# A hybrid decoder layer: where the gate sums, their weights' buffers and a scan's output sums stand in the heads' stage

## Chip, cores, metric

One core of a Trainium2 chip runs the whole layer as one program. The metric is the device time of one execution in microseconds (us); lower is better. Engines are named as in the profile: PE (matrix products; PEld its weight loads), DVE (vector), ACT (scalar), POOL (GpSimd), SP (the queue that issues most transfers).

## What is computed

One layer with 512 tokens and width 2048, in float32: a normalised and modulated input, one wide projection, a sliding-window attention branch, a gated DeltaNet branch, and a gated merge of the two. The change lies in the DeltaNet branch (32 value heads, in pairs that share one of 16 key heads) and in the layer's output gate, which is computed beside it:

```python
mod = jax.nn.silu(c) @ w_ada + b_ada
shift, scale, gate = jnp.split(mod[:, None, :], 3, axis=-1)
...
o = gated_delta_rule(dq, dk, dv, g, beta)
o = rms_norm(o, dn_norm_w) * jax.nn.silu(dz.reshape(B, T, DN_V_HEADS, DN_HEAD_V).astype(f32))
y_b = o.reshape(B, T, DN_VAL).astype(x.dtype) @ w_o_dn
...
return x + gate * (y @ w_out)
```

The product with `w_o_dn` is done with seven products of half-size blocks instead of eight (a Strassen-Winograd scheme). It needs sums of the four quarters of `o` (two heads by two halves of the tokens) as inputs: these are the "input sums" of the change, made by `head_sums`.

## The kernel before

Each projection is a `channel_tile` (line 254 to 256 by its helper `mm3`): 16 blocks of 128 by 128 weights against 512 tokens, each as three products of split numbers (high and low parts). A weight half is copied by ACT (`whi`, line 52) and subtracted by DVE (`wlo`, line 53); `raw` is its load on SP.

The order of everything else hangs on these tiles. After every second block `channel_tile` calls `pump()`, and this document calls one such call a **step**: 8 steps a tile. A piece of side work is a Python generator; it gets a step, issues some instructions, and says with `yield n` after how many steps it wants to go on. `go` puts a generator into the list `live`. `beside(gen, rate)` puts one into a queue that is served after the live ones: its counter grows by `rate` a step and the generator gets a turn for each whole 1.0. The instructions so issued get their place in the program's order. That order is a priority: a scheduler at build time simulates the program and gives each engine the first instruction that is ready, so that one can overtake another. Only generators wrapped in `ordered` (the gate, and the sums of `w_od` that use POOL and SP transfers) are tied behind the last matrix product before them.

`heads(wk, g)` runs for g = 0 to 15, one pair of heads each, with five tiles: the query tile (steps 1 to 8), two value tiles (9 to 16 and 17 to 24) and two output-gate tiles `z` (25 to 32 and 33 to 40). Counted from the `yield`s, a pair's work falls on these steps; numbers over 40 lie in the next pair, 40 lower:

| step | work (line) |
|---|---|
| 9 to 13 | query convolution: 3 DVE products at 10 (595), tanh at 12, DVE at 13 (602) |
| 17 to 21 | the same for the first value tile, `yv`: 595 at 18, tanh (600) at 20, 602 at 21 |
| 19 | POOL's decay masks (792, 794); loads of `qe`, `tt`, `ta`, `lab` |
| 23 | transposes of the first value tile, `ptv` (288), then ACT's copy; POOL's `qe` product (945) |
| 24, 26, 28 | `pqk` with its masks on DVE (951); `py`; `pu` |
| 25 to 31 | the second value tile: 595 at 26, 602 at 29, `ptv` at 31 |
| 33, 41 | first and second `z`: ACT writes `zh` (880) and a tanh |
| 34 to 54 | the scan in four chunks: `pv`, ACT's `vn` (1000), DVE's `vs` (1005), `pd`, `po` (1018) |
| 56, 57 | root of the norm, then two products on `osb` (1048) |
| 59, 60 | transposes `pto` and product into `z` (1055), one per head |
| 61, 65 | the four sums (1064 to 1067) into `osb`; three transfers to `oq_d` (1070) |

Buffers: `z` has two, one per head; `osb` one; the transposes, `pqk`, `py`, `pu` and `pgate` share two banks (`ptp`).

The gate runs from pair 8 on at 0.125 a step: at steps 8, 16, 24, 32 and 40 of every pair. Each of 32 turns multiplies a 128 by 1024 block of weights by a scalar and adds it to a sum (line 1637, DVE), and loads the block two turns ahead into one of two buffers `gw` (1626). Then four times a matrix product `pgate` (1645) and, one turn later, a bias (1647, 1648).

Of the kernel before, what the change touches and what calls it, by code (L numbers as in the profile page):

```python
# [7 lines left out]
F32 = mybir.dt.float32  # L8
# [3 lines left out]
ALU = mybir.AluOpType  # L12
# [4 lines left out]
P = 128  # L17
T = 512
D = 2048
KT = D // P  # L20
# [16 lines left out]
class Layer:  # L37
# [650 lines left out]

    def od_order(self):
        return [  # L690
            ("m1", 0, (0, 0)), ("m2", 1, (1, 0)), ("m5", 3, None), ("m6", 4, None), ("m7", 5, None), ("m4", 2, None),
            ("m3", 6, (1, 1)),
        ]

# [173 lines left out]
    def heads(self, wk, g):  # L868

        st = {"z": []}  # L870
        self.go(self.queries(wk, g, self.channel_tile(f"q{g}"), st), 0)
        for e in range(2):
            self.go(self.values(wk, g, e, self.channel_tile(f"v{2 * g + e}"), st), 0)
        for e in range(2):
            self.go(self.zgate(wk, self.channel_tile(f"z{2 * g + e}"), st), 0)
# [102 lines left out]
    def scan(self, wk, g, k, kT, TT, qd, M, epsq, st):  # L978
# [3 lines left out]
        osb = wk.tile([P, 2, NTB, P], F32, tag="osb", name="osb", bufs=1)  # L982
        osq = wk.tile([P, 2, NTB], F32, tag="osq", name="osq")
        S = None
        for c in range(NTB):
            if c:
# [3 lines left out]
                for e in range(2):  # L990
                    nc.vector.scalar_tensor_tensor(  # L991
                        out=r[:, e, :], in0=pp[:, e, :], scalar=self.neg_eg[:, c, 2 * g + e : 2 * g + e + 1],
                        in1=v[e][:, c, :], op0=ALU.mult, op1=ALU.add,
# [8 lines left out]
            if c < NTB - 1:  # L1002
                vs = wk.tile([P, 2, P], F32, tag="vs", name="vs", bufs=1)
                for e in range(2):
                    nc.vector.tensor_scalar(
                        out=vs[:, e, :], in0=vn[:, e, :], scalar1=self.kd[:, c, 2 * g + e : 2 * g + e + 1],
# [15 lines left out]
            if c < NTB - 1:  # L1022
# [3 lines left out]
                else:  # L1026
                    for e in range(2):
                        nc.vector.scalar_tensor_tensor(
                            out=Sn[:, e, :], in0=S[:, e, :], scalar=self.egl[:, c, 2 * g + e : 2 * g + e + 1],
                            in1=pd[:, e, :], op0=ALU.mult, op1=ALU.add,  # L1030
# [4 lines left out]
        z = st["z"]  # L1035
# [4 lines left out]
        for e in range(2):  # L1040
            nc.vector.scalar_tensor_tensor(
                out=ms[:, e, :], in0=osq[:, e, :], scalar=1.0 / P, in1=epsq, op0=ALU.mult, op1=ALU.add
# [3 lines left out]
        for e in range(2):  # L1046
            of = osb[:, e]
            nc.vector.tensor_tensor(
                out=of, in0=of, in1=ro[:, e * NTB : (e + 1) * NTB].unsqueeze(2).to_broadcast([P, NTB, P]), op=ALU.mult
            )  # L1050
        yield 2
        for e in range(2):
# [1 line left out]
            self.transpose4(pt, lambda c: osb[:, e, c, :])  # L1054
            nc.vector.tensor_tensor(out=z[e], in0=pt, in1=z[e], op=ALU.mult)
            yield 1
        yield from self.head_sums(g, z, osb.rearrange("p e c i -> p (e c i)").rearrange("p (q t) -> p q t", q=4))

    def head_sums(self, g, z, s):

        nc = self.nc
        TT, STT = nc.vector.tensor_tensor, nc.vector.scalar_tensor_tensor
        lo, hi = slice(0, 256), slice(256, 512)
        TT(out=s[:, 0], in0=z[0][:, hi], in1=z[1][:, hi], op=ALU.subtract)
        STT(out=s[:, 1], in0=s[:, 0], scalar=-1.0, in1=z[0][:, lo], op0=ALU.mult, op1=ALU.subtract)
        TT(out=s[:, 2], in0=z[0][:, lo], in1=z[0][:, hi], op=ALU.add)
        STT(out=s[:, 3], in0=s[:, 1], scalar=-1.0, in1=z[1][:, lo], op0=ALU.mult, op1=ALU.subtract)
        yield 4
        for q, src in ((slice(0, 1), z[0][:, lo].unsqueeze(1)), (slice(1, 3), z[1].rearrange("p (q t) -> p q t", q=2)), (slice(3, 7), s)):
            nc.sync.dma_start(out=self.oq_d[q, g // 2].rearrange("q p k t -> p q k t")[:, :, g % 2, :], in_=src)  # L1070


# [545 lines left out]
    def gate(self, wk):  # L1618

        nc, a = self.nc, self.a  # L1620
        acc = wk.tile([P, D], F32, name="gate_bc", bufs=1)
        ws = {}

        def load(i):
            ws[i] = wk.tile([P, 1024], F32, tag="gw", name="gw", bufs=2)
            nc.sync.dma_start(out=ws[i], in_=a["w_ada_gate"][i // 2][:, i % 2 * 1024 : i % 2 * 1024 + 1024])

        load(0)
        load(1)
        for i in range(2 * KT):  # L1630
            yield
            s = self.sc[:, i // 2 : i // 2 + 1]
            o = acc[:, i % 2 * 1024 : i % 2 * 1024 + 1024]
            if i < 2:
                nc.vector.tensor_scalar(out=o, in0=ws.pop(i), scalar1=s, scalar2=None, op0=ALU.mult)
            else:
                nc.vector.scalar_tensor_tensor(out=o, in0=ws.pop(i), scalar=s, in1=o, op0=ALU.mult, op1=ALU.add)
            if i + 2 < 2 * KT:
                load(i + 2)
        for c in range(4):  # L1640
            sl = slice(c * T, (c + 1) * T)
            b = wk.tile([P, T], F32, tag="gb", name="gb", bufs=1)
            nc.sync.dma_start(out=b, in_=a["b_gate"][sl].partition_broadcast(P))
            ps = self.ptp.tile([P, T], F32, tag="tp", name="pgate")
            nc.tensor.matmul(ps, lhsT=self.ones, rhs=acc[:, sl], start=True, stop=True)
            yield
            nc.vector.tensor_tensor(out=acc[:, sl], in0=ps, in1=b, op=ALU.add)
            nc.vector.tensor_scalar(out=acc[:, sl], in0=acc[:, sl], scalar1=0.5, scalar2=None, op0=ALU.mult)
            yield
            nc.sync.dma_start(out=self.gate_d[sl], in_=acc[0:1, sl])  # L1650
# [80 lines left out]
```

## Time and profile before

| | us |
|---|---|
| median of 3 runs | 2895.6 (2894.57 to 2895.92) |
| profiled execution, its own time | 2899.93 |
| its span, first to last instruction | 2898.1 |
| PE busy | 2835.8 |
| DVE busy | 1874.1 |
| ACT busy | 1140.0 |
| POOL busy | 272.5 |

The page's busy times are unions over the span; a line such as "PE ptv L288 <- DVE yv L602" names the instruction that stood, its line, and the one that released it. In the heads' stage the first pair's `pqk` is at 560.1 us of the span and the last one's at 1596.4; the gate's DVE work runs from 1089.3 to 1621.1.

### The profile page before, as it was taken

How to read it: one execution, taken by the hardware profiler on the slowest of the kernel's cores; microseconds unless marked ns; L12 is line 12 of the kernel's file. 1: busy time of each engine (PE TensorE's matmuls, PEld its weight loads, DVE VectorE, ACT ScalarE, POOL GpSimd, SP SyncE). 2: the span in 40 equal slices, each digit the busy share in tenths (PEclk: the TensorE clock that was granted, in tenths of full speed). 3: DMA queues.
4: the chain of work that ended last, by engine and by line, in shares of the span. 5: the costliest groups of instructions: out<-in, count | busy, mean ns of one | idle time of the engine just before them, and what ended most of it. 6: DMA issues, size and time to landing. Idle time of an engine off the chain costs nothing.

```text
span 2898.1 us, 38268 instructions
## 1 busy us (share of the span) xinstructions
PE 2835.8 (98%) x14428; PEld 2324.7 (80%) x14428; DVE 1874.1 (65%) x3020; ACT 1140.0 (39%) x2161; POOL 272.5 (9%) x266
## 2 busy tenths in 40 slices
PE   8899999999999999999999999999999999999999
PEld 6677888888888888888777888888887788788787
DVE  6765899777876656666665456665655655554565
ACT  4355333433334333333333354443344434432343
POOL 0013111101111111112010000000100100000000
PEclk9999999999999999999999999999999999999999
DMA  9756554637667778878772377676645547365575
GB/s 372 295 171 200 173 179 147 209 117 229 190 194 214 235 212 245 242 224 241 247 209 85 127 252 265 240 247 210 218 153 162 157 154 218 119 225 185 185 231 165
DMA packets 205472, 590.08 MB, mean 204 GB/s; under 512 B 74564, under 2 KB 99652, under 8 KB 154088
## 3 DMA queue, kind: packets, MB, share of 16 engines
q1 hardware_dynamic: 195080, 529.44, 53.8%
q0 software_dynamic: 10208, 58.20, 10.3%
q8 instruction: 113, 1.85, 0.3%
q14 instruction: 71, 0.58, 0.1%
HBM read 523.79 MB, written 166.40 MB: 238 GB/s over the span
## 4 chain that ended last, share of the span: by engine, by line
PE 82%; DVE 4%; issue 2%; DMA 2%; ACT 1%; POOL 0%; SPq 0%; DVEq 0%; POOLq 0%; ACTq 0%
PE mm L254 19%; PE mm L256 19%; PE mm L255 19%; PE od L255 3%; PE od L256 3%; PE od L254 3%; PE m L255 2%; PE m L256 2%; PE m L254 2%; PE S L1369 1%; DVE wlo L53 1%; PE pv L998 1%; PE po L1017 1%; PE pP L288 1%; PE O L1420 1%
## 5 line engine op out<-in xcount | busy, mean ns | idle before, releaser
L254 PE MATMUL mm<-hh,whi 128*128 128x512 f32 x2784 | 1134.4, 407 | 2.3 <-ACT whi L52 1.6
L256 PE MATMUL mm<-hh,wlo 128*128 128x512 f32 x2784 | 1091.3, 392 | 1.2 <-DVE wlo L53 1.2
L255 PE MATMUL mm<-hl,whi 128*128 128x512 f32 x2784 | 1089.0, 391 | 0.0
L53 DVE TENSOR_TENSOR wlo<-raw,whi 128x1024 fp32r<-128x1024 f32 (+1 forms) x476 | 590.2, 1242 | 411.2 <-ACT whi L52 401.1
L52 ACT CAST whi<-raw 128x1024 fp32r<-128x1024 f32 (+1 forms) x476 | 495.4, 1044 | 798.0 <-PE mm L255 676.5
L256 PEld LDWEIGHTS mm<-hh,wlo 128*128 128x128 f32 x2784 | 523.5, 188 | 115.7 <-DVE wlo L53 2.1
L254 PEld LDWEIGHTS mm<-hh,whi 128*128 128x128 f32 x2784 | 524.7, 188 | 113.1 <-issue 9.6
L255 PEld LDWEIGHTS mm<-hl,whi 128*128 128x128 f32 x2784 | 525.1, 189 | 99.8 <-issue 1.4
L255 PE MATMUL od<-wlo,oh 128*128 128x512 f32 x448 | 174.7, 390 | 1.0 <-DVE wlo L53 1.0
L254 PE MATMUL od<-whi,oh 128*128 128x512 f32 x448 | 174.9, 391 | 0.0
L256 PE MATMUL od<-whi,ol 128*128 128x512 f32 x448 | 174.4, 389 | 0.0
L792 POOL TENSOR_TENSOR E<-E,neg_g 128x512 f32<-128x512 f32 x64 | 87.4, 1365 | 493.3 <-DMA E<-g_rows 382.1
L945 POOL TENSOR_TENSOR qe<-qe,yq 128x512 f32<-128x512 f32 x32 | 46.0, 1455 | 869.4 <-DMA qe<-eg_rows 749.6
L844 DVE TENSOR_TENSOR A<-A,atmp 128x62 f32<-128x62 f32 (+30 forms) x124 | 113.1, 912 | 1.5
L837 DVE TENSOR_TENSOR atmp<-A 128x62 f32<-128x62 f32 (+30 forms) x124 | 109.5, 883 | 1.4
L255 PEld LDWEIGHTS od<-wlo,oh 128*128 128x128 f32 x448 | 84.1, 188 | 18.7 <-DVE wlo L53 1.6
L254 PEld LDWEIGHTS od<-whi,oh 128*128 128x128 f32 x448 | 84.1, 188 | 17.4 <-ACT whi L52 0.3
L256 PEld LDWEIGHTS od<-whi,ol 128*128 128x128 f32 x448 | 84.1, 188 | 17.4
L53 DVE TENSOR_TENSOR wlo<-raww,whi 128x1024 fp32r<-128x1024 f32 x56 | 68.4, 1223 | 44.1 <-ACT whi L52 44.1
L52 ACT CAST whi<-raww 128x1024 fp32r<-128x1024 f32 x56 | 58.8, 1054 | 79.4 <-PE m L256 71.8
L991 DVE SCALAR_TENSOR_TENSOR r<-pp,neg_eg,vt 128x128 f32<-128x128 f32 x96 | 29.2, 346 | 77.9 <-PE pp L988 77.6
L1393 ACT ACTIVATE sm<-sm,mx,rs 128x256 f32<-128x256 f32 (+1 forms) x128 | 71.7, 562 | 3.3 <-DVE mx L1388 3.3
(341 smaller groups left out, 3273.9 us busy)
## 6 DMA issues: line engine op xcount, KB each, us to landing
raw<-in_w_ch SPq DMA_DIRECT2D x158, 1024.0 KB
wa<-in_w_ada_ss SPq DMA_DIRECT2D x32, 1024.0 KB
od_m<-in_w_od POOLq DMA_DIRECT2D x32, 1024.0 KB, 13.5
raw<-od_m SPq DMA_DIRECT2D x32, 1024.0 KB
raw<-in_w_od SPq DMA_DIRECT2D x24, 1024.0 KB
E<-g_rows SPq DMA_DIRECT2D x64, 256.0 KB
od_m<-in_w_od SPq DMA_DIRECT2D x16, 1024.0 KB
od_m<-od_m SPq DMA_DIRECT2D x16, 1024.0 KB
```

The lines of the kernel that those rows point to most:

```text
L52: self.nc.scalar.copy(out=hi, in_=src)
L53: self.nc.vector.tensor_tensor(out=lo, in0=src, in1=hi.bitcast(F32), op=ALU.subtract)
L254: nc.tensor.matmul(ps, lhsT=wh, rhs=xh, start=first, stop=False)
L255: nc.tensor.matmul(ps, lhsT=wh, rhs=xl, start=False, stop=False)
L256: self.last_mm = nc.tensor.matmul(ps, lhsT=wl, rhs=xh, start=False, stop=last).ins
L288: self.nc.tensor.transpose(dst[:, c * P : (c + 1) * P], src_cols(c), self.ident)
L792: self.in_turn(nc.gpsimd.tensor_tensor(out=E, in0=E, in1=ng, op=ALU.add))
L837: eng.tensor_tensor(out=t, in0=A[:, m : m + 1, m + 1 :].to_broadcast([P, m, n]), in1=A[:, :m, m : m + 1].to_broadcast([P, m, n]), op=ALU.mult,
L844: eng.tensor_tensor(out=A[:, :m, m + 1 :], in0=A[:, :m, m + 1 :], in1=t, op=ALU.add)
L945: self.in_turn(nc.gpsimd.tensor_tensor(out=qf, in0=qf, in1=q, op=ALU.mult))
L991: nc.vector.scalar_tensor_tensor(out=r[:, e, :], in0=pp[:, e, :], scalar=self.neg_eg[:, c, 2 * g + e : 2 * g + e + 1], in1=v[e][:, c, :], ...
L1393: nc.scalar.activation(t, t, AF.Exp, scale=r[:, h : h + 1], bias=mx[:, h : h + 1], accum_out=den[:, h : h + 1])
```

## The change

It has three parts. `heads` sets the rate of the gate's queue to 0 at the start of each pair and to 0.22 before the second value tile, so that the gate gets turns only in steps 17 to 40; its weights get three buffers and are loaded three turns ahead, and its bias takes one of these buffers. Ten steps are put between the last transpose of a scan's output and the four sums, which then fall on steps 71 and 72 (31 and 32 of the next pair), their transfers on 75 (35). And the sums go into a tile of their own with three parts (`zs`), the fourth into `z[0]` itself; the seven inputs get a new order in `oq_d`, and `od_order` names them by it.

```diff
-            ("m1", 0, (0, 0)), ("m2", 1, (1, 0)), ("m5", 3, None), ("m6", 4, None), ("m7", 5, None), ("m4", 2, None),
+            ("m1", 0, (0, 0)), ("m2", 2, (1, 0)), ("m5", 4, None), ("m6", 5, None), ("m7", 1, None), ("m4", 3, None),
...
         st = {"z": []}
+        for q in self.side.get("gate", []):
+            q[1] = 0.0
         self.go(self.queries(wk, g, self.channel_tile(f"q{g}"), st), 0)
         for e in range(2):
+            for q in self.side.get("gate", []) if e else []:
+                q[1] = 0.22
             self.go(self.values(wk, g, e, self.channel_tile(f"v{2 * g + e}"), st), 0)
...
-        yield from self.head_sums(g, z, osb.rearrange("p e c i -> p (e c i)").rearrange("p (q t) -> p q t", q=4))
-
-    def head_sums(self, g, z, s):
+        yield 10
+        yield from self.head_sums(wk, g, z)
+
+    def head_sums(self, wk, g, z):
...
+        s = wk.tile([P, 3, 256], F32, tag="sums", name="zs", bufs=1)
         TT(out=s[:, 0], in0=z[0][:, hi], in1=z[1][:, hi], op=ALU.subtract)
         STT(out=s[:, 1], in0=s[:, 0], scalar=-1.0, in1=z[0][:, lo], op0=ALU.mult, op1=ALU.subtract)
-        TT(out=s[:, 2], in0=z[0][:, lo], in1=z[0][:, hi], op=ALU.add)
-        STT(out=s[:, 3], in0=s[:, 1], scalar=-1.0, in1=z[1][:, lo], op0=ALU.mult, op1=ALU.subtract)
-        yield 4
-        for q, src in ((slice(0, 1), z[0][:, lo].unsqueeze(1)), (slice(1, 3), z[1].rearrange("p (q t) -> p q t", q=2)), (slice(3, 7), s)):
+        yield 1
+        TT(out=z[0][:, hi], in0=z[0][:, lo], in1=z[0][:, hi], op=ALU.add)
+        STT(out=s[:, 2], in0=s[:, 1], scalar=-1.0, in1=z[1][:, lo], op0=ALU.mult, op1=ALU.subtract)
+        yield 3
+        two = lambda x: x.rearrange("p (q t) -> p q t", q=2)
+        for q, src in ((slice(0, 2), two(z[0])), (slice(2, 4), two(z[1])), (slice(4, 7), s)):
             nc.sync.dma_start(out=self.oq_d[q, g // 2].rearrange("q p k t -> p q k t")[:, :, g % 2, :], in_=src)
...
-            ws[i] = wk.tile([P, 1024], F32, tag="gw", name="gw", bufs=2)
+            ws[i] = wk.tile([P, 1024], F32, tag="gw", name="gw", bufs=3)
...
-        load(0)
-        load(1)
+        for i in range(3):
+            load(i)
...
-            if i + 2 < 2 * KT:
-                load(i + 2)
+            if i + 3 < 2 * KT:
+                load(i + 3)
...
-            b = wk.tile([P, T], F32, tag="gb", name="gb", bufs=1)
+            b = wk.tile([P, 1024], F32, tag="gw", name="gb", bufs=3)[:, :T]
```

## The prediction

> **What bounds the kernel now.** I read the page first, then the matrix engine's waits in the stage that the change touches, then stretches cut from one query-key product (pqk) to the next, which is one pair of heads, and last the order of instructions on DVE, ACT and SP inside a pair.
>
> ```profile
> span 2898.1 us, 38268 instructions
> PE 2835.8 (98%) x14428; PEld 2324.7 (80%) x14428; DVE 1874.1 (65%) x3020; ACT 1140.0 (39%) x2161; POOL 272.5 (9%) x266
> PE 82%; DVE 4%; issue 2%; DMA 2%; ACT 1%; POOL 0%; SPq 0%; DVEq 0%; POOLq 0%; ACTq 0%
> ```
>
> PE works 98% of the span. The change takes no matrix product away, so it can only win back time in which PE waits or is slow. The waits of PE from 1033 to 1680 us (line waited for: us in total, times, longest):
>
> ```profile
> PE ptv L288 <- DVE yv L602: 11.6, 6, 2.6
> PE pto L288 <- DVE zh L1055: 2.2, 1, 2.2
> PE pto L288 <- DVE osb L1048: 1.3, 1, 1.3
> ```
>
> Six times PE stands at the transposes of the first value tile (ptv) until DVE has finished that tile's activation (yv, line 602). The stretches (length, then busy time of PE, PEld, DVE, ACT, POOL, clock, DMA):
>
> ```profile
> 763.14:830.45 67.31, 67.31 (x359) 56.04 (x358) 55.54 (x86) 24.81 (x57) 10.97 (x10) 1.00 0.66 195
> 1033.62:1172.67 139.05, 136.51 (x714) 113.29 (x714) 83.83 (x141) 50.01 (x113) 17.33 (x17) 0.99 0.79 233
> 1172.67:1241.87 69.20, 67.50 (x358) 55.96 (x358) 42.78 (x72) 24.95 (x57) 8.61 (x8) 1.00 0.81 241
> 1241.87:1310.78 68.91, 67.47 (x358) 55.94 (x358) 42.67 (x72) 25.04 (x57) 9.91 (x9) 1.00 0.72 227
> 1310.78:1380.61 69.83, 67.46 (x359) 55.96 (x358) 44.35 (x73) 25.14 (x57) 9.31 (x9) 1.00 0.83 244
> 1380.61:1449.17 68.56, 67.47 (x358) 55.95 (x358) 42.34 (x71) 25.03 (x57) 5.86 (x7) 1.00 0.78 248
> 1449.17:1520.89 71.72, 69.08 (x359) 57.22 (x358) 45.81 (x74) 26.02 (x59) 12.67 (x11) 0.98 0.74 207
> 1520.89:1595.77 74.88, 72.64 (x365) 58.68 (x364) 39.95 (x73) 23.79 (x55) 2.53 (x2) 0.98 0.28 94
> 1168.50:1173.00 4.50, 3.92 (x15) 3.37 (x16) 2.40 (x4) 1.31 (x2) 0.00 (x0) 0.62 1.01 215
> 1517.00:1521.50 4.50, 4.21 (x17) 3.66 (x18) 2.10 (x4) 1.56 (x3) 0.00 (x0) 0.62 0.92 313
> ```
>
> A pair without the gate's sums takes 67.31 us and PE never stops. With them, the seven pairs in rows two to seven take 139.05 + 69.20 + 68.91 + 69.83 + 68.56 + 71.72 = 487.27 us against 7 x 67.31 = 471.17: 16.1 us too many. 11.6 of it is the six waits. The granted clock is 0.62 over 4.5 us at two of them, 0.38 x 4.5 = 1.7 us each, 3.4 together; the rest, 1.1, is small. The ceiling of the main effect is 16.1 us, 0.56%. The eighth pair (1520.89) has 7.6 us extra: the 2.2 of the pto wait, slow clock and the gate's own matrix products.
>
> The clock drops behind waits of at most 2.6 us. The Trainium skill, "TensorE: Matmul & The Clock Gate", section "Part 1: The HAM clock gate", says that the clock halves after an idle window of about 3.4 us. By that rule the drops would not hang on these waits, and the forecast below would be 3.4 us higher; the trace has both drops right at two of the six waits, and I follow the trace. By the rule it would be 2887.3 in place of 2883.9.
>
> **The change part by part.** One pair is 40 steps of 67.31 / 40 = 1.68 us. Why L602 is late, in the pair of 1310.78 (DVE, POOL, then PE):
>
> ```profile
> 1365.88 0.69 DVE L1048 TENSOR_TENSOR osb<-osb,roy 128x512 f32<-128x512 f32 x1
> 1366.49 1.28 DVE L1637 SCALAR_TENSOR_TENSOR gate_bc<-gw,silu_c,gate_bc 128x1024 f32<-128x1024 f32 x1
> 1367.69 1.78 DVE L1048 TENSOR_TENSOR osb<-osb,roy 128x512 f32<-128x512 f32 x1
> ...
> 1374.71 1.08 DVE L1066 TENSOR_TENSOR osb<-zh 128x256 f32<-128x256 f32 x1
> 1375.71 0.68 DVE L1055 TENSOR_TENSOR zh<-pto,zh 128x512 f32<-128x512 f32 x1
> 1376.31 1.21 DVE L53 TENSOR_TENSOR wlo<-raw,whi 128x1024 fp32r<-128x1024 f32 x1
> 1377.44 0.41 DVE L1064 TENSOR_TENSOR osb<-zh 128x256 f32<-128x256 f32 x1
> 1377.78 0.68 DVE L602 SCALAR_TENSOR_TENSOR yv<-th,yv 128x512 f32<-128x512 f32 x1
> 1367.60 3.01 POOL L945 TENSOR_TENSOR qe<-qe,yq 128x512 f32<-128x512 f32 x2 [57.29 <-DMA qe<-eg_rows]
> 1378.60 0.63 PE L288 MATMUL ptv<-ident,yv 128*128 128x128 f32 x4 [2.37 <-DVE yv L602]
> ```
>
> PE is there at 1378.60 - 2.37 = 1376.23, 10.35 us after the first osb; L602 ends 12.58 after it, with a gate sum (1.20 start to start) and two input sums (1.00 and 0.34) ahead. A pair without a gate sum:
>
> ```profile
> 1021.43 1.29 DVE L1048 TENSOR_TENSOR osb<-osb,roy 128x512 f32<-128x512 f32 x2
> 1026.92 1.15 DVE L602 SCALAR_TENSOR_TENSOR yv<-th,yv 128x512 f32<-128x512 f32 x1 [0.16 <-ACT th L600]
> 1031.63 0.60 PE L288 MATMUL ptv<-ident,yv 128*128 128x128 f32 x4
> ```
>
> There L602 ends 6.64 after the first osb and PE comes 3.56 us later.
>
> *Gate sums.* None falls at step 16 any more. At 0.22 a step, counted from step 17, the first of a pair comes at steps 21, 20, 19, 17, 21, 19, 18, 17 of the eight pairs. At 21 it is written after L602, at 17 to 20 still ahead of it. *Input sums.* Ten more steps put them from step 21 to 31 and 32 in the program's order, behind both tiles' L602 (21 and 29). But the order on each engine is made by a scheduler that runs what is ready, and nothing ties these sums to their step, so I expect them right behind L602, where DVE had them in pairs without a gate sum. What they delay there is the mask of pqk at step 24; DVE has room for it, busy 42 to 46 of some 69 us in the stretches above.
>
> For the quoted pair: 12.58 - 1.34 = 11.24 with a gate sum still ahead, 10.04 with none. Against 10.35, PE waits 0.9 or nothing. The other bound is the pair at 1021.43: 6.64 and even a gate sum of 1.20 added is 2.5 us early, because once the backlog is gone L602 overtakes the second wlo. Five pairs of the waiting six have their gate sum at 17 to 20: 0 to 4.5 us left. I take 1.0, nearer to the second row, since a pair that has neither a gate sum at step 16 nor input sums ahead of L602 starts out as that pair does. Gain 16.1 - 1.0 = 15.1.
>
> The second osb above takes 1.78 instead of 0.69 us beside POOL's qe. The Trainium skill, "SBUF — State Buffer", section "SBUF: two separate sides", says that a DVE instruction with two SBUF inputs and a GpSimd instruction exclude each other for the whole instruction; the row agrees. It speaks against the new place, which lies in POOL's burst: the second rival.
>
> *Output buffers.* The sums now read z and write into z[0]; the transfers of z[0] wait for the third sum. z has two buffers, and the next pair's zh takes the first at step 33, though the transfers are written at step 35. The place of the present last transfer, behind the sums, shows what to expect (SP, ACT, DVE; then who waited for it):
>
> ```profile
> 1310.62 0.37 SPq L1070 DMA_DIRECT2D oq_d<-osb  x1
> 1325.48 0.69 ACT L880 ACTIVATE zh<-mm,dnwh 128x512 f32<-128x512 f32 x1
> 1328.35 0.48 DVE L1005 TENSOR_SCALAR vs<-vn,kd 128x128 f32<-128x128 f32 x2 [0.91 <-ACT vn L1000]
> 1331.12 0.42 DVE L1025 COPY S<-pd 128x256 f32<-128x256 f32 x1 [2.29 <-PE pd L1013]
> 1331.57 0.37 ACT L1018 COPY osb<-po 128x256 f32<-128x256 f32 x1
>   ACT osb L1018: 2.9, 1
> ```
>
> That transfer has until 1331.57 and was late once, by 2.9 us. zh is due 6.1 us earlier, so the worst pair could hold ACT for 9.0 us. Queued on ACT behind zh: its tanh, vn of the scan, the next weight cast. vs, and PE's pd behind it, have about 2.5 us to spare (idle 0.91 and part of 2.29). So 0 to 6.5 us for a pair, 0 to 97 for fifteen pairs. Fourteen of fifteen transfers met the later term and z[0]'s is ahead of most of the bytes: I take one or two pairs, 2.5 us. On SP it must get ahead of the loads that follow the products of step 26, or it stands behind these 9.6 us:
>
> ```profile
> 1316.36 4.83 SPq L932 DMA_DIRECT2D ta<-ta_d  x1
> 1321.23 4.77 SPq L933 DMA_DIRECT2D lab<-lab_d  x1
> ```
>
> *Weights of the gate sums.* Same 32 loads and the same bytes, bunched in 24 steps of 40, issued three sums ahead. DVE waited for them hardly at all:
>
> ```profile
> DVE gate_bc L1637 <- DMA gw<-in_w_ada_gate: 0.5, 1, 0.5
> ```
>
> The load-to-use distance shrinks from 16 steps (26.9 us) to 13 or 14 (about 22), in the first pair to 5 (8.4). A late one blocks DVE with wlo and the second L602 behind it: 0 to 6 us, I take 0.9. What it can save is that 0.5. The reordered rows of the scratch tensor move the same bytes in three transfers: nothing. The gate's last products still hold one of two transpose buffers at steps 19 and 20 of the eighth pair, so the 2.2 us pto wait stays; if not, it comes back with its slow clock, 0.02 x 74.88 = 1.5, together 3.7.
>
> Sum: -16.1 + 1.0 + 2.5 + 0.9 = -11.7. The profiled execution took 2899.93, so 2888.2 for it; the median of the three runs is 4.3 lower, 2895.6, and 2895.6 - 11.7 = 2883.9.
>
> **The rivals.** *A: the output buffers decide (slower).* From the point where z[0]'s transfers land more than 2.5 us after zh is due, as when the sums slip past step 26 and SP is held. For it: the one late transfer, DMA shares of 0.66 to 0.83. Against: fourteen met a term only 6.1 us later, and zh can wait in the scheduler's order. Eight pairs at 3 us on PE: 24 more than nothing, 2895.6 - 15.1 + 0.9 + 24 = 2905.
>
> *B: the gate sum meets POOL's burst ahead of L602.* Now and then it does already (min/median/max in ns):
>
> ```profile
> L1637 DVE SCALAR_TENSOR_TENSOR gate_bc<-gw,silu_c,gate_bc x30: 1265/1277/2118, 1112.4 to 1517.9; 128x1024 f32<-128x1024 f32 x30
> ```
>
> A sum at steps 17 to 20 waits for a POOL instruction, 3.01 / 2 = 1.5 us, and five pairs keep 0.9 + 1.5 = 2.4 us, less what shrinks of the other overlaps, say 1.6: 8 us, one clock drop with it. -16.1 + 9.7 + 2 = -4.4: 2891. That is also the sum by the page's rule on the shared port. Against: 3.56 us of slack in the row at 1031.63.
>
> *C: the order hardly changes*, since the scheduler hoists the sums ahead of L602 wherever its tanh is late: 2894.
>
> **How the numbers follow.** About 0.2%, 5.8 us, is what a measurement of this kernel can tell from no change. Forecast 0.57, A 0.18, B 0.15, C 0.10. The forecast's own range is 2876 (all 19.8 us back: 16.1 + 3.7) to 2890. Up to 2900 it takes in B, C and a mild A. Faster: 0.57 and two thirds of B, 0.67; same: the rest of B, and C, 0.15; slower: A, 0.18.
>
> **What would show it.** Right: the pairs after 1033 take 67.3 to 67.8 us, the ptv row is gone from PE's waits or below 2 us, the clock is 1.00 there, the four sums stand behind L602. Wrong: a row of ACT zh waiting for the oq_d transfer with PE pd waiting for vs behind it (A), ptv waits of 1 to 2 us with a stretched gate sum ahead (B), sums still ahead of L602 (C), or waits at pqk, py or pu that are not there now.

## The result, and the profile after

| | median (lowest to highest), us | against before, 95% interval |
|---|---|---|
| before, 8 runs | 2895.02 (2891.92 to 2899.24) | |
| after, 8 runs | 2883.93 (2880.12 to 2893.21) | 0.9964 [0.9952, 0.9975] |

The medians are 11.1 us apart; the ratio of the runs says 0.36% less. The profiled execution of after took 2883.98 us, that of before 2899.93: these two are 15.95 apart. The point by point section comes back to the difference.

The page of after, its span, its busy times and its chain:

```profile
span 2882.2 us, 38250 instructions
...
PE 2831.3 (98%) x14428; PEld 2320.8 (81%) x14428; DVE 1869.0 (65%) x3020; ACT 1138.6 (40%) x2161; POOL 277.2 (10%) x266
...
PE 85%; DVE 2%; issue 2%; DMA 2%; ACT 1%; POOL 0%; SPq 0%; DVEq 0%; POOLq 0%; ACTq 0%
```

The share of DVE in the chain fell from 4% to 2%, and PE's rose from 82% to 85%. The span is shorter by 15.9 us, though DVE's busy time is only 5.1 less: what changed is above all when DVE works.

PE's waits in after from 1033 to 1680 us (line waited for: us in total, times, longest):

```profile
PE pto L288 <- DVE zh L1059: 2.2, 1, 2.2
PE pto L288 <- DVE osb L1052: 1.3, 1, 1.3
PE ptv L288 <- DVE yv L602: 0.9, 2, 0.6
PE pu L967 <- DVE Y L963: 0.7, 1, 0.7
PE py L961 <- issue: 0.6, 1, 0.6
PE pv L1002 <- DVE r L995: 0.2, 1, 0.2
```

The row of ptv was 11.6 us in six waits and is 0.9 in two. The last three rows come to 1.5 us. The pto row of 2.2 is still there. The stretches of after, cut as before from one pqk to the next:

```profile
1033.38:1168.00 134.62, 134.62 (x714) 112.06 (x713) 79.50 (x137) 49.79 (x113) 18.41 (x18) 1.00 0.79 238
1168.00:1236.09 68.09, 67.47 (x357) 55.95 (x356) 43.83 (x76) 25.01 (x57) 9.15 (x9) 1.00 0.79 240
1236.09:1303.55 67.46, 67.46 (x358) 55.95 (x356) 42.09 (x70) 25.03 (x57) 9.06 (x8) 1.00 0.77 240
1303.55:1370.86 67.31, 67.31 (x358) 56.03 (x357) 43.82 (x74) 25.00 (x57) 11.14 (x11) 1.00 0.84 247
1370.86:1438.22 67.36, 67.36 (x357) 55.95 (x356) 42.95 (x73) 24.90 (x57) 8.54 (x8) 1.00 0.82 259
1438.22:1508.41 70.19, 68.95 (x360) 56.38 (x358) 43.34 (x73) 25.82 (x59) 10.50 (x10) 1.00 0.69 196
1508.41:1580.70 72.29, 69.43 (x361) 56.84 (x360) 41.41 (x77) 23.96 (x55) 2.53 (x2) 1.00 0.33 107
```

The first two pairs take 134.62 = 2 x 67.31 us: PE never stops there, with the gate's sums beside it. Five of the first six pairs are within 0.2 us of 67.31, the other has one ptv wait of 0.6. The granted clock is 1.00 in every row. The first two of the gate's eight pgate products now lie at the end of the seventh pair (70.19).

All eight pairs in one stretch, before and then after (the columns are those of the stretches above):

```profile
1033.62:1595.77 562.15, 548.14 (x2856) 453.00 (x2856) 341.73 (x574) 199.98 (x449) 66.23 (x61) 0.99 0.71 215
```

```profile
1033.38:1580.70 547.32, 542.60 (x2855) 449.16 (x2854) 336.93 (x574) 199.52 (x449) 69.34 (x62) 1.00 0.72 220
```

The stage is 14.83 us shorter. PE's idle time fell from 562.15 - 548.14 = 14.01 to 4.72, a gain of 9.29. PE's busy time fell by 5.54 for the same products. Before had three stretches at half clock here (at 1169, 1517 and 1589 us), after has none, so one comes to about 5.54 / 3 = 1.85 us.

Last, DVE in after, in the pair of 1303.55 (start, us, engine, line, operation):

```profile
1291.35 1.29 DVE L1052 TENSOR_TENSOR osb<-osb,roy 128x512 f32<-128x512 f32 x2
...
1299.70 1.84 DVE L602 SCALAR_TENSOR_TENSOR yv<-th,yv 128x512 f32<-128x512 f32 x1
1301.47 1.65 DVE L1645 SCALAR_TENSOR_TENSOR gate_bc<-gw,silu_c,gate_bc 128x1024 f32<-128x1024 f32 x1
1303.04 1.27 DVE L1070 TENSOR_TENSOR zs<-zh 128x256 f32<-128x256 f32 x1
1304.34 0.73 DVE L1071 SCALAR_TENSOR_TENSOR zs<-zs,zh 128x256 f32<-128x256 f32 x1
1305.00 0.41 DVE L1073 TENSOR_TENSOR zh<-zh 128x256 f32<-128x256 f32 x1
1305.33 0.41 DVE L1074 SCALAR_TENSOR_TENSOR zs<-zs,zh 128x256 f32<-128x256 f32 x1
```

The four sums stand right behind L602 and one gate sum, not ten steps (16.8 us) behind their old place: the scheduler pulled them forward. No input sum stands ahead of L602 in any pair of after from 950 to 1600 us. L602 itself takes 1.84 us here in place of 0.68, and ends 10.19 us after the first osb (1301.54 - 1291.35). That is only 0.16 us inside the 10.35 us that the prediction took from before, and PE does not wait for ptv in this pair.

### The profile page after: what moved, and what is told of

Its sections match the earlier page's. It is cut to its first block, busy times and chain, and to the rows that moved or that the text cites. A ratio compares the mean times of both kernels' runs of the same rounds, so it can differ in the third digit from the quotient of the medians.

```text
span 2882.2 us, 38250 instructions
## 1 busy us (share of the span) xinstructions
PE 2831.3 (98%) x14428; PEld 2320.8 (81%) x14428; DVE 1869.0 (65%) x3020; ACT 1138.6 (40%) x2161; POOL 277.2 (10%) x266
## 3 DMA queue, kind: packets, MB, share of 16 engines
q0 software_dynamic: 10208, 58.20, 10.2%
q8 instruction: 113, 1.85, 0.3%
## 4 chain that ended last, share of the span: by engine, by line
PE 85%; DVE 2%; issue 2%; DMA 2%; ACT 1%; POOL 0%; SPq 0%; DVEq 0%; POOLq 0%; ACTq 0%
PE mm L254 20%; PE mm L256 20%; PE mm L255 20%; PE od L254 3%; PE od L255 3%; PE od L256 3%; PE m L255 2%; PE m L256 2%; PE m L254 2%; PE S L1377 1%; PE pv L1002 1%; PE po L1021 1%; PE O L1428 1%; PE pP L288 1%; PE po L1020 1%
```

## The experiments

The theory was: the six ptv waits come from DVE's backlog ahead of L602, both parts of the change shorten it, and the third buffer and the wait for the output buffers are side costs. The rivals were that the output buffers cost PE time (A), that the gate's sums alone do it all, and that the ten steps do nothing. The gate's part with three buffers, and the input sums left where they were, was not run. The first four kernels ran beside 15 runs of before (median 2896.7, 2893.0 to 2901.74), the last four beside 11 (2896.07, 2890.2 to 2903.78).

**The gate's part alone, with two buffers.** Before, with only this:

```diff
+        for q in self.side.get("gate", []):
+            q[1] = 0.0
...
+            for q in self.side.get("gate", []) if e else []:
+                q[1] = 0.22
```

> The kernel before with the gate's rates alone (0, then 0.22 from the second value tile on); input sums and two buffers as before. Theory 1, each of the two parts takes about half of the DVE backlog ahead of L602: the ptv waits shrink from 11.6 us to 3 to 5, since 1.34 us of input sums still stand ahead of L602 in the five pairs that have a gate sum at steps 17 to 20; time 2886 to 2889, ratio 0.997 to 0.998. Theory 2, the gate sum at step 16 alone makes the backlog: ptv waits under 1 us, time 2884, ratio 0.996. Theory 3, the input sums alone do: no change, 2895.

Measured: 2923.21 (2920.29 to 2926.82), ratio 1.0092 [1.0078, 1.0106]. It is slower by 26.5 us; no theory had that. Waits of PE and of DVE in this kernel, 1033 to 1680 us:

```profile
PE pd L1017 <- DVE vs L1009: 22.0, 4, 8.4
PE pu L967 <- DVE Y L963: 6.8, 2, 6.4
...
PE ptv L288 <- DVE yv L602: 1.9, 3, 0.8
```

```profile
DVE gate_bc L1641 <- DMA gw<-in_w_ada_gate: 41.6, 9, 9.9
...
DVE gate_bc L1639 <- DMA gw<-in_w_ada_gate: 7.4, 1, 7.4
```

The aim is met, ptv falls from 11.6 to 1.9, but DVE stands 49.0 us for the gate's weights. The longest case, on SP, then DVE, then PE:

```profile
1485.70 2.05 SPq L1630 DMA_DIRECT2D gw<-in_w_ada_gate  x1
...
1492.65 1.28 DVE L1641 SCALAR_TENSOR_TENSOR gate_bc<-gw,silu_c,gate_bc 128x1024 f32<-128x1024 f32 x1 [9.87 <-DMA gw<-in_w_ada_gate]
...
1494.45 0.48 DVE L1009 TENSOR_SCALAR vs<-vn,kd 128x128 f32<-128x128 f32 x2
...
1494.98 1.22 PE L1017 MATMUL pd<-vs,k 128*128 128x256 f32 x2 [8.40 <-DVE vs L1009]
...
1498.14 0.63 PE L254 MATMUL mm<-hh,whi 128*128 128x512 f32 x1
...
1499.71 0.40 PE L255 MATMUL mm<-hl,whi 128*128 128x512 f32 x1
```

The load is issued at 1485.70, after a load of lab has held SP for 9.80 us, and the sum that uses it starts at 1492.65, after DVE has stood 9.87 us. vs is queued behind that sum on DVE, and PE's pd behind vs: 8.40 us. After it PE's products take 0.63 us, as the one at 1498.14, and from about 1499.7 again 0.40: the half clock. Turns every 1 / 0.22 = 4.5 steps, 7.6 us, and a lead of two turns leave 15 us from load to use where before had 26.9.

**The sums' part alone.** Before, with `yield 10`, the tile `zs` and the new order; the gate stays at 0.125 with two buffers:

```diff
+        yield 10
+        yield from self.head_sums(wk, g, z)
...
+        s = wk.tile([P, 3, 256], F32, tag="sums", name="zs", bufs=1)
```

> The kernel before with the input sums' part alone (ten steps, a tile of their own, new order in oq_d); gate at 0.125 a step with two buffers. Theory 1: L602 ends 11.2 us after the first osb where PE comes after 10.35, so about 0.9 us of wait in six pairs, 5 us in all; time 2887 to 2890, ratio 0.997 to 0.9985. Theory 2 (the gate sum at step 16 is all): ptv waits 9 to 12 us, time 2894 to 2896. Theory 3 (the input sums are all): waits under 1 us, time 2884.

Measured: 2888.39 (2887.7 to 2896.63), ratio 0.9979 [0.997, 0.9988]. That is 8.3 us faster by the medians, 0.21% by the ratio. Six of its eleven times lie from 2887.7 to 2888.39, the other five from 2891.53 to 2896.63, and the execution that left the trace is one of the slow ones, 2895.87. PE's waits in it, 1033 to 1680 us:

```profile
PE ptv L288 <- DVE yv L602: 6.9, 5, 2.6
...
PE pu L963 <- DVE Y L959: 1.6, 2, 1.3
...
PE pd L1013 <- DVE vs L1005: 1.2, 1, 1.2
```

The time is that of the first theory. In this trace the sums are worth 11.6 - 6.9 = 4.7 us of ptv, less than the 11.6 - 1.9 = 9.7 of the gate's part alone, and 2.8 us of waits for pu and vs (the last two rows) take back part of it; how much of this holds for the faster executions is not shown. So each part shortens the waits by itself. What the sums add in time once the gate's part has its three buffers is not shown.

**The whole change without the ten steps.**

```diff
-        yield 10
         yield from self.head_sums(wk, g, z)
```

> The changed kernel without the ten steps: the input sums are written at steps 61 and 62 again, in their own tile. Theory 1, the ten steps work through the place in the order alone and let L602 ahead of the sums where a gate sum stands at 17 to 20: one or two sums return ahead of L602 in those pairs, ptv waits 2 to 4 us in place of 0.9, time 2885 to 2888, 0.0005 to 0.0015 slower than the changed kernel. Rival, the ten steps do nothing because the sums need z of the second head, which comes just ahead of L602 anyway: same order, same time, 2884.

Measured: 2885.4 (2883.85 to 2886.38), ratio 0.996 [0.9947, 0.9972]. The times do not tell it from after; the waits differ, in the same stretch:

```profile
PE ptv L288 <- DVE yv L602: 3.8, 4, 1.7
```

One place on DVE in this kernel shows why:

```profile
1231.76 1.27 DVE L1069 TENSOR_TENSOR zs<-zh 128x256 f32<-128x256 f32 x1
1232.95 1.11 DVE L602 SCALAR_TENSOR_TENSOR yv<-th,yv 128x512 f32<-128x512 f32 x1
```

One input sum, stretched to 1.27 us, is ahead of L602 again, as in three of the four waits. In these two traces the ten steps are worth the 2.9 us of ptv between 3.8 and 0.9.

**The sums held at their steps.** After, with the four sums tied behind the last matrix product ahead of them by the kernel's own helper, so that they really run at steps 31 and 32:

```diff
-        TT(out=s[:, 0], in0=z[0][:, hi], in1=z[1][:, hi], op=ALU.subtract)
+        with self.behind():
+            TT(out=s[:, 0], in0=z[0][:, hi], in1=z[1][:, hi], op=ALU.subtract)
...
```

> The changed kernel with the four sums tied behind the last matrix product of their steps (31 and 32 of the next pair), so that the scheduler cannot run them early. Rival A of the prediction at full size: z[0]'s transfer is then issued behind the loads of ta and lab, zh stands for it 3 to 9 us in most pairs and PE's pd behind it; 1 to 4 us in each of 15 pairs, time 2900 to 2940, ratio 1.002 to 1.015. If the scheduler moves zh back in ACT's order as well, or the transfers land in time anyhow: 2883 to 2887, and rival A had no ground.

Measured: 2881.71 (2880.43 to 2887.13), ratio 0.9955 [0.9941, 0.9968]. The 2900 to 2940 of rival A did not come. ACT's wait for the output buffers from 1033 to 1680 us, in after and then in this kernel, and this kernel's waits of PE:

```profile
ACT zh L884 <- DMA oq_d<-zh: 2.2, 1, 2.2
```

```profile
ACT zh L884 <- DMA oq_d<-zh: 10.5, 5, 3.4
```

```profile
...
PE ptv L288 <- DVE yv L602: 0.6, 1, 0.6
PE pd L1017 <- DVE vs L1009: 0.3, 1, 0.3
```

The wait that rival A describes is made five times as large as in after (10.5 us in place of 2.2), in five pairs. PE stands 0.3 us behind vs, and no other row of its waits grew.

**The whole change with two buffers.** After, with the weights' buffers and lead of before, and a buffer of its own for the bias again:

```diff
-            ws[i] = wk.tile([P, 1024], F32, tag="gw", name="gw", bufs=3)
+            ws[i] = wk.tile([P, 1024], F32, tag="gw", name="gw", bufs=2)
...
-            if i + 3 < 2 * KT:
-                load(i + 3)
+            if i + 2 < 2 * KT:
+                load(i + 2)
...
```

> The changed kernel with two buffers for the gate's weights, loaded two turns ahead as before, everything else as changed. Theory after the run of the rates alone: turns 4 to 5 steps apart and a load only two turns ahead leave about 9 steps, 15 us, where loads take longer in the middle of a pair; DVE stands in order for 40 to 50 us in all and PE behind it for 20 to 30: time 2908 to 2920, ratio 1.004 to 1.009. Rival, the 2923 came from the input sums ahead of L602 together with the bunched gate sums: then two buffers cost little here, 2884 to 2890.

Measured: 2903.17 (2899.91 to 2907.63), ratio 1.0026 [1.0014, 1.0038]. It is 7.1 us slower than the runs of before beside it, where after was 11.1 faster: 18.2 us between them. The time lies between the two ranges expected. The largest wait of DVE for the weights and the largest of PE, 1033 to 1680 us:

```profile
DVE gate_bc L1645 <- DMA gw<-in_w_ada_gate: 35.4, 8, 9.4
```

```profile
PE pd L1017 <- DVE vs L1009: 14.8, 4, 7.9
```

So the change needs the third buffer with its longer lead: without them the sign turns. This kernel is still some 19 us faster than the gate's part alone; what of that is due to the input sums, which stand ahead of L602 there, was not taken apart.

**No gate sums at all.** Before, with 30 of the 32 sums on DVE left out; loads and matrix products stay (its gate is no longer the layer's, so it is no kernel to use):

```diff
-                nc.vector.scalar_tensor_tensor(out=o, in0=ws.pop(i), scalar=s, in1=o, op0=ALU.mult, op1=ALU.add)
+                ws.pop(i)
```

> The kernel before with 30 of the gate's 32 DVE sums left out (their loads stay), so the gate is not that of the reference. Ceiling of the main effect: pairs 9 to 15 take 67.3 us each, no ptv wait over 0.7, time 2878 to 2882, ratio 0.9945 to 0.996. If the waits had another cause in the second half of the stage (loads, transfers), they stay and the time is above 2890.

Measured: 2881.76 (2880.84 to 2883.52), ratio 0.9954 [0.994, 0.9968]. This is what the gate's sums on DVE cost before: 14.3 us by the medians. PE's ptv waits are not among its rows for 1033 to 1680 us, though the input sums stand where they were: without gate sums PE does not wait for L602. The interval overlaps that of after: the whole change hides most of this cost.

**Before once more, with a profile.**

> The kernel before, unchanged, for a second profile. Theory: its waits are the same 11 to 12 us of ptv and 2.2 of pto each time, but how many of them the clock follows with a slow stretch of 1.7 us differs from run to run (three in the first profile): span 2892 to 2898, with 0 to 3 slow stretches between 1100 and 1600 us. If the slow stretches belong to fixed waits, there are three again and the span is 2897 to 2899.

Measured: one time of 2899.31 us, span 2897.5. PE's waits, 1033 to 1680 us:

```profile
PE ptv L288 <- DVE yv L602: 11.6, 6, 2.6
PE pto L288 <- DVE zh L1055: 2.1, 1, 2.1
```

The waits come back, six with the same sum. Half clock came at 1238, 1378, 1518 and 1590 us: four times, where zero to three were expected, and partly at other waits, so the drops are not tied to fixed waits.

**A better version.** Tied sums, and each pgate product in the same turn as its bias, so that it does not hold a transpose buffer for a turn (the diff is to the tied kernel):

```diff
+            yield
...
-            yield
```

> The kernel with tied sums, and the gate's last four products issued in the same turn as their bias, so that a pgate holds its transpose bank for about 2 us and not for 4 to 5 steps. Theory: the one pto wait of 2.2 us in the last pair but one is the bank that pgate holds: it goes, time 2878 to 2881, 1 to 3 us faster than tied (2881.7). Rival, DVE's backlog alone makes that wait: it stays at 2.2, time 2881 to 2883.

Measured: 2879.28 (2876.79 to 2880.08), ratio 0.9943 [0.993, 0.9955], the lowest median of all. PE's waits, here from 480 to 1720 us:

```profile
PE pd L1017 <- DVE vs L1009: 1.8, 2, 1.5
PE ptv L288 <- DVE yv L602: 1.5, 3, 0.7
PE pto L288 <- DVE osb L1052: 1.3, 1, 1.3
```

The pto wait of 2.1 to 2.2 us, in every other trace of this study, is gone, as the theory had it. Its slowest run (2880.08) is just below the fastest of after (2880.12), but the intervals of the two ratios still touch, and that of the tied kernel overlaps widely: no time tells it from that one.

## Why the prediction was right

Forecast 2883.9, measured 2883.93. The mechanism was right, but the closeness is largely luck: several terms were off and cancelled.

*The main effect.* Right in kind, and the size came out by another way. The prediction left 1.0 us of the ptv waits, the trace shows 0.9. But the prediction took 1.0 because a pair with a gate sum ahead of L602 would be 2.5 us early (6.64 + 1.20). In after four pairs have such a sum; there L602 ends 10.10, 10.19, 10.51 and 10.82 us after the first osb, around the 10.35 at which PE comes. That is nearer to the prediction's other bound, 11.24, and the two above 10.35 make the 0.9. The prediction put the sums right behind L602 rather than at their steps, and there they are. Undoing a part brings the waits back: 3.8 without the ten steps, 6.9 without the gate's part.

*The ceiling of 16.1.* Slightly wrong. The prediction set the stretches against 7 x 67.31 us and called what was left over small. After keeps 475.03 - 471.17 = 3.86 us over it in seven pairs (1508.41 - 1033.38 = 475.03). Of that, 0.9 is ptv and 0.9 are new waits for pu and pv. Most of the remainder is the gate's own products: 68.95 us of PE work in the seventh pair against 67.31. Before had them in the eighth pair. So the seven pairs gave 487.27 - 475.03 = 12.24 us where 15.1 was forecast, and the eighth gave 74.88 - 72.29 = 2.59 where nothing was.

*Output buffers, 2.5.* The step is mis-sized: PE pays nothing that shows. ACT stood for them twice in the whole of after:

```profile
  DMA oq_d<-zh: 3.4, 2
```

"One or two pairs" was right. But the 2.5 us that vs and pd have to spare, which the prediction itself had read, cover a wait of this length: the price counted ACT's wait as PE's. The tied kernel shows it for a larger wait, so rival A's mechanism exists, and for 10.5 us of it, at most 3.4 in a pair, PE paid no more than 0.3.

*The gate's weights, 0.9.* DVE waits more than before, 5.5 us in two. SP and then DVE and PE in after:

```profile
1447.59 10.80 SPq L937 DMA_DIRECT2D lab<-lab_d  x1
...
1459.17 0.57 SPq L1634 DMA_DIRECT2D gw<-in_w_ada_gate  x1
...
1464.57 1.28 DVE L1645 SCALAR_TENSOR_TENSOR gate_bc<-gw,silu_c,gate_bc 128x1024 f32<-128x1024 f32 x1 [3.35 <-DMA gw<-in_w_ada_gate]
```

The load stands behind lab's 10.80 us on SP, comes 3.35 us late, and PE waits 0.2 for it (the pv row). So 0.9 was too much for three buffers. What the prediction did not see is how near the edge this is: with two buffers and the shorter lead the time is 18 us longer, three times the 6 us at which the prediction closed its bounds. That bound thought of one late load; with two buffers DVE stood for nine (eight in the row shown there, and one of 3.4 us at another line).

*The mask behind the hoisted sums.* "DVE has room for it" held but once, for 0.7 us: the pu wait at 1446.30, where four sums, a gate sum and wlo lie ahead of the masks and of Y. The four sums take 1.27, 1.15, 0.85 and 1.27 us there, against 0.41 each in a pair of the tied kernel.

*The clock.* The two drops at ptv waits went, as the prediction took from the trace against the page's rule; by that rule the time would have been 2887.3. A third drop went too, behind a pto wait that did not change: 2.24 us before, 2.25 after. That was not forecast. The same wait has a drop in six of the nine traces that have it; which ones is a matter of when it falls, as the last section shows. So this part of the gain, about 1.85 us, is luck of the one profiled execution.

*From the profile to the median.* The sum of 11.7 was made for the profiled execution, for which it gave 2888.2; it took 2883.98, a gain of 15.95: 9.29 of waits, 5.54 of clock, 1.1 outside the eight pairs, whose cause was not followed. The medians differ by 11.1. Before's profiled executions took 2899.93 and 2899.31, its medians were 2895.02 to 2896.7; after's profiled one lay on its median. Only profiled executions leave a trace, so what the others do differently stays open. A hint is the clock: beside the last four kernels, before took 2890.2 us at a mean granted clock of 0.998, 2894.72 at 0.997 and 2903.78 at 0.993, so its time moves with its clock; the two traces of before have three and four drops in the eight pairs. The costs that did not come (2.5 + 0.9) and the gain that did not reach the median cancel.

*The rivals.* A: its wait came, within the time that vs and pd have to spare. C did not occur. B did, in small: both ptv waits that are left have no input sum but a stretched gate sum ahead of L602, of 2.13 and of 1.73 us. The longer one, DVE and then PE in after:

```profile
1227.14 2.13 DVE L1645 SCALAR_TENSOR_TENSOR gate_bc<-gw,silu_c,gate_bc 128x1024 f32<-128x1024 f32 x1
...
1234.25 0.63 PE L288 MATMUL ptv<-ident,yv 128*128 128x128 f32 x4 [0.62 <-DVE yv L602]
```

The slack of 3.56 us that the prediction held against B is not there in the four pairs with a gate sum ahead: two have 0.16 and 0.25 us left (10.35 less 10.19 and 10.10), two have none. B's price at ptv was the 0.9 us that is left, and not the 8 that it was given.

## What to carry to other kernels

Work that is bunched into a part of a loop needs its loads further ahead in turns, because the turns come closer together: count the lead in microseconds and set it against the longest hold on the issuing queue. A wait on an engine beside the bottleneck has a price only beyond the slack of what is queued behind it, so read that slack before pricing the wait. Where a scheduler takes whatever is ready, a delay written in steps only lowers a priority: say where the instruction will land, and not where it was written.

## What the runs showed of the hardware

PE's clock fell to half after waits of about 2 us, and not each time. In the ten traces, between 480 and 1720 us, PE had 24 waits of 1.97 us or more; 20 were followed, or overlapped, by a stretch at half clock, of 3.4, 6.8 or 10.2 us. The four without are 2.37 us (before), 2.25 (after), 2.19 (without the ten steps) and 2.16 (tied). None of 27 waits from 1.00 to 1.92 us had one. The Trainium skill, "TensorE: Matmul & The Clock Gate", section "Part 1: The HAM clock gate", gives windows of about 3.4 us for going down and for coming back: the lengths of the stretches agree with it, but waits of 1.97 to 2.64 us, shorter than such a window, brought the clock down 13 times of 17 here.

The place of the wait accounts for the rest. Within each trace, stretches of half clock start at multiples of 3.413 us from one another. If each trace is cut into windows on this grid, the stretch from 480 to 1720 us gives, in ten traces, 3597 windows at full clock. In 20 of them PE stands 1.96 us or more, and half clock follows every one; it follows none of the others, which have at most 1.92. A wait that lies across a border counts in two parts (idle is the window's length less PE's busy time):

| trace | window, us | PE idle, us | clock in the next window |
|---|---|---|---|
| before, ptv wait of 2.37 | 1165.75 to 1169.16 | 2.37 | 0.50 |
| before, ptv wait of 2.37 | 1373.96 to 1377.37 | 1.13 | 1.00 |
| | 1377.37 to 1380.78 | 1.23 | 1.00 |
| before, pto wait of 2.24 | 1585.59 to 1589.01 | 1.96 | 0.50 |
| after, pto wait of 2.25 | 1569.26 to 1572.68 | 0.67 | 1.00 |
| | 1572.68 to 1576.09 | 1.58 | 1.00 |

The grid lies differently in the ten traces, so that one wait of 2.2 us costs a drop in one execution and none in another. The bound is that of this stage: ahead of 480 us nine drops followed windows with 1.50 to 1.87 us of idle time, and why was not followed.

A small load on SP held its queue for 10.80 us once (lab in after, above), longer than the 7.6 us between two turns of the gate; the 32 loads of lab there have a median of 0.61.
